# Turning v in 32x32 blocks on VectorE instead of TensorE, with adaLN rows loaded a step ahead and residual rows parked in DRAM

## Chip, cores, metric

The kernel runs on one core of a Trainium2 chip. The metric is the device time of one execution in microseconds (us). The core has TensorE (PE; its weight loads are shown apart as PEld), VectorE (DVE), ScalarE (ACT), GpSimd (POOL) and SyncE (SP). SP and ACT also issue DMAs, each on a queue of its own; an engine takes its instructions in order, so a DMA issue that waits holds up what stands behind it.

## What is computed

The reference is a backbone of two layers over 256 latent tokens that attend after 256 context tokens (512 together), model width 1024. Layer 0 mixes tokens by a Conformer convolution, layer 1 by a bidirectional mLSTM with 4 heads of 512. A squared-ReLU MLP of width 4096 follows in each layer, and shift, scale and gate of each half come from an adaLN map of a conditioning vector. All is float32. Cut to the part around the change:

```python
def adaln(cvec, w, b):
    return jnp.split(jax.nn.silu(cvec) @ w + b, 6, axis=-1)

def mlstm_features(u, ...):                     # MLSTM_INNER = 2048
    up = u @ w_up
    xm, z = up[..., :MLSTM_INNER], up[..., MLSTM_INNER:]
    xc = jax.nn.silu(dwconv(xm, w_conv) + b_conv)
    q, k, v = xc @ w_q, xc @ w_k, xm @ w_v
    gates = jnp.concatenate([q, k, v], axis=-1) @ w_gate + b_gate
    o = jax.nn.sigmoid(xm @ w_o + b_o)
    return xc, z, q, k, v, gates, o

# layer: x <- LN(ALPHA*x + gate * mixer(...)), then
h = layer_norm(ALPHA * h + g2 * sq_relu_mlp(modulate(h, sh2, sc2), ...), ...)
```

The scan then needs v with the tokens as rows (`scores @ v`, `k.T @ v` in chunks of 128 tokens).

## The kernel before

**Products.** Features lie on the 128 partitions and the 512 tokens in the free dimension. A float32 product is made of three fp32r matmuls: operands are split into a rounded part and a rest, and hi x hi, lo x hi and hi x lo are summed (`mm3` at L181, L184, L185; `mm3t`, with the operands exchanged, at L212 to L214; `mm_any` at L196, L197). Weights come from DRAM in tiles of 1 MB (`raw_load`, L144, on SP's queue, three buffers). ScalarE casts half a tile to `wh` (L150) and VectorE subtracts to get `wl` (L151); four pairs of them are in turn.

**Order.** A scheduler puts the instructions of every engine in one fixed order by dependencies and a model of costs; buffers come from pools, so a tile waits for the last reader of the buffer it reuses. Each DMA raises one of eight semaphores in turn, and an issue waits for the older DMA on its own one.

**The v stage** (about 719 to 926 us) computes v = xm @ w_v in 16 blocks of 128 output features, two at a time. `v_epi(m)` copies the finished block from PSUM to `vt` (ScalarE, L1215). Two blocks later `v_out` turns it: four transposes of 128x128 by TensorE into the PSUM tile `ln` (L1227), a ScalarE copy to `E` (L1229), and a store of 256 KB to `v_dr` in DRAM (L1230, ScalarE's queue). After every fourth block, so once a head, four gate matmuls per group (`gate_acc`, L1206) add v's part of the gates. Between the blocks of v stand the matmuls of w_q's transpose with the gate weights (`wgq_step`, L756), which end in a copy to `F` (L761) and transposes (L764). The q stage behind it begins with halves of `xc`, loaded, cast and split.

**adaLN rows.** `AdaV.step` multiplies rows of the adaLN map by the conditioning vector on VectorE: it loads a row tile `ar` of 256 KB (L418, SP's queue, one buffer, 80 times) and multiplies and adds it for each stream (L422 the first time, L426 afterwards). The first set runs during layer 0's MLP, the second (`ada_n2`) during v, q and k.

**Residual rows.** `R` (tile `res`, 128 x 2 x 1024, 1 MB) is filled by four ScalarE copies at 631 to 635 us (L1172). It is next read at 1354 us, when the mLSTM's down projection adds to it (L1648). The attention, with the o gates' weights (`gate_o`, `raw<-wo`), stands from about 1205 to 1475 us, then the second MLP.

Of the kernel before, what the change touches and what calls it, by code (L numbers as in the profile page):

```python
# [14 lines left out]
P = 128  # L15
# [7 lines left out]
H = 4  # L23
# [48 lines left out]
def hybrid_kernel(ctx: ExitStack, tc: tile.TileContext, xT, vecs_d, wdw_d, ada0_w, ada_w, wg_d, pw1a, pw1, pw2, w1_0, w2_0,  # L72
# [12 lines left out]
    def nm(s):  # L85
        uid[0] += 1
        return f"{s}_{uid[0]}"
# [3 lines left out]
    def tmp(tag, dt=F32):  # L91
        return tp.tile([P, T], dt, tag=tag, name=nm(tag), bufs={"E": 4, "S": 2, "L": 2, "F": 1}[tag])
# [8 lines left out]
    def psum(tag="mm"):  # L101
        return pp.tile([P, 512], F32, tag=tag, name=nm(tag), bufs={"mm": 3, "ln": 2, "fl": 1, "cv": 2}[tag])
# [297 lines left out]
    class AdaV:  # L400
# [3 lines left out]

        def __init__(self, l, units, streams, rows=()):
            self.l, self.units, self.streams, self.i, self.acc, self.todo = l, list(units) + list(rows), streams, 0, [], []
            self.ncol = len(units)

        def step(self):
            if self.todo:  # L410
                self.todo.pop(0)()
            n, kt = divmod(self.i, DT)
            if n == len(self.units):
                return
            if kt == 0:
                self.acc += [tmp("SL"[(len(self.acc) + i) // 2 % 2]) for i in range(len(self.streams))]
            w = adp.tile([P, 512], F32, tag="ar", name=nm("ar"))
            nc.sync.dma_start(w, ada_w[self.l, self.units[n], kt // 4, :, kt % 4 * 512:kt % 4 * 512 + 512])  # L418
            for i, s in enumerate(self.streams):
                a, c = self.acc[i - len(self.streams)], cs[:, kt, 14 + s:15 + s]  # L420
                if kt == 0:
                    o = nc.vector.tensor_scalar(a, w, c, None, op0=ALU.mult)  # L422
                    if i == 0:
                        tc.keep_in_program_order(o)
                else:
                    nc.vector.scalar_tensor_tensor(a, w, c, a, op0=ALU.mult, op1=ALU.add)  # L426
            self.i += 1
            if kt == DT - 1 and n < self.ncol and len(self.acc) == 4:
                accs, self.acc = self.acc, []
                u = self.units[n] + 1 - 4 // len(self.streams)  # L430
                self.todo += [lambda: self.sums(accs), lambda: None, lambda: self.end(u)]

        def flush(self):
            while self.todo:
# [725 lines left out]
    for _ in side:  # L1160
        pass

    R = xp.tile([P, 2, D], F32, name="res")
    for f in range(0, DT, 2):
        t, tr = tmp("S"), psum("cv")
        for i in range(2):
            nc.scalar.activation(t[:, i * C:(i + 1) * C], x[f + i][:, HI], AF.Identity, scale=al[:, 0, f + i:f + i + 1],
                                 bias=al[:, 1, f + i:f + i + 1])
            for tt in range(2):
                nc.tensor.transpose(tr[:, tt * C + i * P:tt * C + (i + 1) * P],  # L1170
                                    t[:, i * C + tt * P:i * C + (tt + 1) * P], ident)
        nc.scalar.copy(R[:, :, f * P:(f + 2) * P], tr.rearrange("p (t c) -> p t c", t=2))  # L1172

    xm = []

# [32 lines left out]
        seen.add(j)  # L1208

    wgv = gate_w(2, qc.tile([P, T], F32, name="wgv"))  # L1210
    vts = []

    def v_epi(m, ps):
        vt = B("vt").rearrange("p a b -> p (a b)")[:, :T]
# [6 lines left out]
    def v_out(m, vt):  # L1221
        if m % 4 == 3:
            for j in range(4):
                gate_acc(j, wgv[:, m - 3 + j, :], vts[m - 3 + j])
        tr = psum("ln")
        for b in range(4):
            nc.tensor.transpose(tr[:, b * P:(b + 1) * P], vt[:, b * P:(b + 1) * P], ident)  # L1227
        vk = tmp("E")
        nc.scalar.copy(vk, tr)  # L1229
        nc.scalar.dma_start(v_dr[m // 4][:, :, (m % 4) * P:(m % 4 + 1) * P], vk.rearrange("p (b c) -> p b c", b=4))  # L1230

    late = []

# [218 lines left out]
    def rows(dst, src):  # L1452
        nc.sync.dma_start(dst, src.broadcast_to([P, dst.shape[-1]]))
        return dst


    HF = [slice(0, 512), slice(512, 1024)]
    G1 = rows(qe.tile([P, D], F32, name="G1"), rows_d[0:1])
    for i in range(2):
        ada_n2.row(i, G1[:, HF[i]])  # L1460
    pw = {}
# [65 lines left out]
    def gate_o(h):  # L1527

        for d in range(2):
            bo = rows(BO().rearrange("p a b -> p (a b)"), bo_d[h:h + 1, d * DH:(d + 1) * DH])  # L1530
            pss = [psum() for _ in range(2)]
            for q in range(4):
                ws = preo if (h, d, q) == (0, 0, 0) else None
                if ws is None:
                    raw = raw_load(wo[h, d, q])
                for i in range(2):
                    w = ws[i] if ws else split_w(raw[:, i * 1024:(i + 1) * 1024])
                    for t in range(2):
                        for k in range(2):
                            kt = 4 * q + 2 * i + k  # L1540
                            sl = slice(k * 512, (k + 1) * 512)
                            mm3t(pss[t], xls[kt][0][:, BLK[t]], xls[kt][1][:, BLK[t]], w[0][:, sl], w[1][:, sl],
                                 kt == 0, kt == ET - 1)
                        if q == 3 and i == 1:
                            og[h, d, t] = o_ = OG()
                            nc.vector.tensor_tensor(o_, pss[t], bo, op=ALU.add)
                            nc.scalar.activation(o_, o_, AF.Sigmoid)
                    yield
# [368 lines left out]
    return v.reshape(-1, P).T  # L1917


def _layout(np, i):  # L1920
    g = {k: np.asarray(v) for k, v in i.items()}
    a = {}
    a["xT"] = np.concatenate([g["ctx"][0], g["x"][0]], axis=0).T
    vec = {
        "c_ctx": _cols(g["c_ctx"]), "c": _cols(g["c"][0]),
        "b_pw1": _cols(g["conv_b_pw1"][0]),
        "cln_g": _cols(g["conv_ln_g"][0]), "cln_b": _cols(g["conv_ln_b"][0]),
        "b_pw2": _cols(g["conv_b_pw2"][0]), "b_conv": _cols(g["ml_b_conv"][0]),
        "w_conv": g["ml_w_conv"][0].T.reshape(ET, P, QTAP).transpose(1, 0, 2).reshape(P, ET * QTAP),
        "gn_g": _cols(g["ml_gn_g"][0]), "skip": _cols(g["ml_skip"][0]),  # L1930
        "b_gate": np.tile(g["ml_b_gate"][0], (P, 4)),
    }
    for l in range(2):
        vec[f"ada_b{l}"] = _cols(g["ada_b"][l])
        for n in ("ln1_g", "ln1_b", "ln2_g", "ln2_b"):
            vec[f"{n}{l}"] = _cols(g[n][l])
    a["vecs_d"] = np.concatenate([vec[n] for n, _ in _VECS], axis=1)
    a["wdw_d"] = np.concatenate([g["conv_w_dw"][0], g["conv_b_dw"][0][None]], axis=0)
    aw = g["ada_w"].reshape(2, DT, P, 6 * D)
    a["ada_w"] = aw.reshape(2, 2, 4, P, 12, 512).transpose(0, 4, 1, 3, 2, 5).reshape(2, 12, 2, P, 2048)  # L1940
    a["ada0_w"] = aw[0, :, :, :2 * D].reshape(DT, P, 2, DT, P).transpose(3, 1, 0, 2, 4).reshape(DT, P, 2048)
    a["wg_d"] = g["ml_w_gate"][0].reshape(3, ET, P, 16).transpose(0, 2, 1, 3).reshape(3, P, 256)
    pw1 = g["conv_w_pw1"][0].reshape(D, 2, DT, P).transpose(0, 2, 1, 3)[:, :, ::-1, :].reshape(D, 2 * D)
    a["pw1a"] = pw1[:, :512].reshape(DT, P, 512)
    a["pw1"] = _blocks(pw1[:, 512:])
    a["pw2"] = _blocks(g["conv_w_pw2"][0])
    for l in range(2):
        a[f"w1_{l}"] = _blocks(g["mlp_w1"][l])
        a[f"w2_{l}"] = np.stack([_blocks(g["mlp_w2"][l][c * D:(c + 1) * D]) for c in range(4)])
    a["up_x"] = _blocks(g["ml_w_up"][0][:, :E])  # L1950
    a["up_z"] = _blocks(g["ml_w_up"][0][:, E:])
    a["wv"] = _blocks(g["ml_w_v"][0])
    a["wo"] = g["ml_w_o"][0].reshape(4, 4, P, 2, H, DH).transpose(4, 3, 0, 2, 1, 5).reshape(H, 2, 4, P, 2048)
    a["bo_d"] = g["ml_b_o"][0].reshape(2, H, DH).transpose(1, 0, 2).reshape(H, 2 * DH)
    a["wk"] = (g["ml_w_k"][0].T.reshape(2, 2, 4, P, 8, 2, P).transpose(0, 4, 3, 1, 5, 2, 6).reshape(2, 8, P, 2048))
    a["wq"] = _blocks(g["ml_w_q"][0])
    a["wqT"] = g["ml_w_q"][0].T.reshape(ET, P, E)
    a["wdown"] = g["ml_w_down"][0].reshape(H, 4, P, 2, 512).transpose(0, 3, 2, 1, 4).reshape(H, 2, P, 2048)
    a["w2_1"] = g["mlp_w2"][1].reshape(16, 2, P, D).transpose(0, 2, 1, 3).reshape(16, P, 2048)
    ab = g["ada_b"][1].reshape(6, D)  # L1960
    a["rows_d"] = np.stack([ab[2], ab[5], g["ln1_g"][1], g["ln1_b"][1], g["ln2_g"][1], g["ln2_b"][1]])
    return {k: np.ascontiguousarray(v) for k, v in a.items()}
# [23 lines left out]
```

## Time and profile before

| | before |
|---|---|
| median of 3 runs | 1670.03 us (1669.85 to 1670.98) |
| profiled execution | 1670.06 us |
| its span, first to last instruction | 1668.3 us |
| granted TensorE clock | 0.998 |
| TensorE busy | 1656.0 us, 8920 instructions |
| VectorE busy | 1030.2 us, 1857 instructions |
| ScalarE busy | 742.2 us, 1196 instructions |
| read from and written to DRAM | 284.37 MB and 15.77 MB |

A row of an engine's groups reads: line, engine, operation, output<-inputs, shape, count. A row of a waits view reads: engine and line that waited <- what it waited for: us in total, times, longest. Rows of a timeline or of the chain begin with the start and the length in us; a row with "x8" stands for eight instructions in a row, and its length for all of them. Matmuls overlap in TensorE, so the sum of their lengths is more than the time they take.

### The profile page before, as it was taken

The page shows a single profiled execution, that of the slowest core. Times are in us where ns is not written, and L with a number is a line of the kernel's source. Part 1 is how long each engine was busy: PE and PEld are TensorE (multiplying, and loading weights), DVE is VectorE, ACT ScalarE, POOL GpSimd, SP SyncE. Part 2 cuts the span into 40 slices and gives each one's busy share as a digit, 9 for nine tenths or more (in the row PEclk, how much of TensorE's full clock was granted, in tenths as well). Part 3 has the DMA queues.
Part 4 walks back from the last instruction along what each step waited for, and adds up shares of the span by engine and source line. Part 5 has one row for each costly group of instructions (what it writes and reads, how often), then busy time and mean ns, then how long its engine had stood idle before and what let it go on. Part 6 is the DMA issues. An engine that isn't in the chain of part 4 may idle for free.

```text
span 1668.3 us, 22876 instructions
## 1 busy us (share of the span) xinstructions
PE 1656.0 (99%) x8920; PEld 1364.9 (82%) x8920; DVE 1030.2 (62%) x1857; ACT 742.2 (44%) x1196; POOL 14.3 (1%) x64
## 2 busy tenths in 40 slices
PE   9999999999999999999999999999999999999998
PEld 6665898888888998877788899888878888878887
DVE  6555895666635765761143663564389876786677
ACT  4313573232324476652243532442368654655453
POOL 0000000000000000000000000000000000000001
PEclk9999999999999999999999999999999999999999
DMA  9565223444324064556775743455375556675552
GB/s 359 201 216 208 85 75 114 151 145 136 136 101 152 10 233 160 185 194 251 266 259 174 259 171 120 143 198 175 130 246 190 192 213 213 253 274 190 179 186 92
DMA packets 73901, 301.63 MB, mean 181 GB/s; under 512 B 7518, under 2 KB 23682, under 8 KB 43968
## 3 DMA queue, kind: packets, MB, share of 16 engines
q1 hardware_dynamic: 56080, 285.44, 48.3%
q10 hardware_dynamic: 17712, 14.72, 2.6%
q8 instruction: 70, 1.15, 0.3%
q14 instruction: 39, 0.32, 0.1%
HBM read 284.37 MB, written 15.77 MB: 180 GB/s over the span
## 4 chain that ended last, share of the span: by engine, by line
PE 96%; DVE 2%; DMA 1%; issue 0%; ACT 0%; SPq 0%; ACTq 0%; DVEq 0%
PE mm L181 17%; PE mm L184 17%; PE mm L185 17%; PE mm L196 7%; PE mm L212 4%; PE mm L214 4%; PE mm L213 4%; PE mm L197 4%; PE cv L212 2%; PE cv L214 2%; PE cv L213 2%; PE fl L343 1%; PE ln L181 1%; PE cv L839 1%; PE ln L184 1%; PE ln L185 1%
## 5 line engine op out<-in xcount | busy, mean ns | idle before, releaser
L151 DVE TENSOR_TENSOR wl<-raw,wh 128x1024 fp32r<-128x1024 f32 x344 | 418.9, 1222 | 276.2 <-ACT wh L150 263.5
L150 ACT CAST wh<-raw 128x1024 fp32r<-128x1024 f32 x344 | 358.7, 1051 | 502.3 <-PE mm L184 278.3
L184 PE MATMUL mm<-u,wh 128*128 128x512 f32 (+1 forms) x808 | 291.6, 361 | 0.2 <-DVE u L594 0.2
L181 PE MATMUL mm<-u,wh 128*128 128x512 f32 (+1 forms) x680 | 243.6, 359 | 0.0
L185 PE MATMUL mm<-u,wl 128*128 128x512 f32 (+1 forms) x680 | 241.3, 355 | 0.0
L184 PEld LDWEIGHTS mm<-u,wh 128*128 128x128 f32 x808 | 152.6, 189 | 22.2 <-DVE u L594 0.5
L181 PEld LDWEIGHTS mm<-u,wh 128*128 128x128 f32 x680 | 128.4, 189 | 25.2 <-issue 5.9
L185 PEld LDWEIGHTS mm<-u,wl 128*128 128x128 f32 x680 | 128.4, 189 | 18.6 <-issue 0.8
L212 PE MATMUL mm<-wh,xl 128*128 128x512 f32 x256 | 101.0, 395 | 0.1
L181 PE MATMUL mm<-xm,wh 128*128 128x512 f32 x256 | 101.0, 394 | 0.0
L213 PE MATMUL mm<-wh,xl 128*128 128x512 f32 x256 | 100.0, 391 | 0.0
L185 PE MATMUL mm<-xm,wl 128*128 128x512 f32 x256 | 99.7, 390 | 0.0
L214 PE MATMUL mm<-wl,xl 128*128 128x512 f32 x256 | 99.2, 391 | 0.0
L181 PE MATMUL mm<-hid,wh 128*128 128x512 f32 (+1 forms) x256 | 93.3, 364 | 0.0
L185 PE MATMUL mm<-hid,wl 128*128 128x512 f32 (+1 forms) x256 | 92.8, 363 | 0.0
L184 PE MATMUL mm<-hid,wh 128*128 128x512 f32 (+1 forms) x256 | 92.8, 363 | 0.0
L196 PE MATMUL mm<-x,wh 128*128 128x512 f32 x232 | 81.1, 398 | 0.0
L426 DVE SCALAR_TENSOR_TENSOR S<-ar,cs,S 128x512 f32<-128x512 f32 x56 | 40.8, 749 | 59.4 <-DMA ar<-ada_w 59.2
L184 PE MATMUL mm<-qq,wh 128*128 128x272 f32 x256 | 73.9, 289 | 0.0
L181 PE MATMUL mm<-qq,wh 128*128 128x272 f32 x256 | 73.5, 288 | 0.0
L185 PE MATMUL mm<-qq,wl 128*128 128x272 f32 x256 | 73.5, 288 | 0.0
L196 PE MATMUL mm<-u,wh 128*128 128x512 f32 x192 | 68.7, 399 | 0.0
(535 smaller groups left out, 3253.2 us busy)
## 6 DMA issues: line engine op xcount, KB each, us to landing
raw<-w SPq DMA_DIRECT2D x64, 1024.0 KB, 4.8
raw<-wo SPq DMA_DIRECT2D x32, 1024.0 KB, 4.8
raw<-ada_w SPq DMA_DIRECT2D x22, 1024.0 KB, 6.5
ar<-ada_w SPq DMA_DIRECT2D x80, 256.0 KB, 3.7
raw<-wv SPq DMA_DIRECT2D x16, 1024.0 KB, 6.8
raw<-wqT SPq DMA_DIRECT2D x16, 1024.0 KB, 6.2
raw<-wq SPq DMA_DIRECT2D x16, 1024.0 KB, 4.9
raw<-wk SPq DMA_DIRECT2D x16, 1024.0 KB, 5.1
```

What stands on the lines that cost most here:

```text
L150: c = nc.scalar.copy(hi, src)
L151: lastsub[0] = nc.vector.tensor_tensor(lo, src, hi.bitcast(F32), op=ALU.subtract).ins
L181: a = nc.tensor.matmul(ps, wh, xh, start=start, stop=False)
L184: nc.tensor.matmul(ps, wh, xl, start=False, stop=False)
L185: lastmm[0] = nc.tensor.matmul(ps, wl, xh, start=False, stop=stop).ins
L196: todo = [lambda s_, e_: nc.tensor.matmul(ps, wh, r[0], start=s_, stop=e_), lambda s_, e_: nc.tensor.matmul(ps[:, :n], wl, r[0][:, :n], st ...
L197: lambda s_, e_: nc.tensor.matmul(ps[:, :n], wl, r[0][:, :n], start=s_, stop=e_)]
L212: nc.tensor.matmul(ps, xh, wh, start=start, stop=False)
L213: nc.tensor.matmul(ps, xl, wh, start=False, stop=False)
L214: nc.tensor.matmul(ps, xh, wl, start=False, stop=stop)
L343: a = mark_unit[0] = nc.tensor.matmul(ps[32 * j:32 * j + 32], cs[:, kt, 14 - 2 * v:46 - 2 * v], blocks[kt], start=first and kt < 4, stop=l ...
L426: nc.vector.scalar_tensor_tensor(a, w, c, a, op0=ALU.mult, op1=ALU.add)
```

## The change

Three things change.

1. v is no longer turned by TensorE. VectorE turns each `vt` block of 128x512 in blocks of 32x32 within the four groups of 32 partitions, directly into a tile `res` of 1 MB that holds one head. After the head's fourth block four DMAs, each from 32 partitions and of 256 KB, store it to `v_dr`. So that a 32x32 turn gives whole rows, the host permutes the columns of w_v within each head, and the rows of w_gate that belong to v. 64 transposes and 16 ScalarE copies are gone.
2. `AdaV.step` loads the next row tile before it uses the present one; `ar` has two buffers.
3. `R` is stored to DRAM (`r_dr`) after it is filled, so that the one `res` buffer can serve v, and loaded again on SP's queue in the first `gate_o`, behind its first weight tile.

```diff
 # class AdaV, step and load
-            n, kt = divmod(self.i, DT)
+            n, kt = divmod(self.i - len(self.loads), DT)
...
-            w = adp.tile([P, 512], F32, tag="ar", name=nm("ar"))
-            nc.sync.dma_start(w, ada_w[self.l, self.units[n], kt // 4, :, kt % 4 * 512:kt % 4 * 512 + 512])
+            w = self.loads.pop(0) if self.loads else self.load()
+            if self.i < DT * len(self.units):
+                self.loads.append(self.load())
...
-            self.i += 1
...
+        def load(self):
+            n, kt = divmod(self.i, DT)
+            w = adp.tile([P, 512], F32, tag="ar", name=nm("ar"), bufs=2)
+            nc.sync.dma_start(w, ada_w[self.l, self.units[n], kt // 4, :, kt % 4 * 512:kt % 4 * 512 + 512])
+            self.i += 1
+            return w

 # residual rows
-    R = xp.tile([P, 2, D], F32, name="res")
+    def rows_tile():
+        return xp.tile([P, 2, D], F32, tag="res", name=nm("res"), bufs=1)
+
+    r_dr = dp.tile([P, 2, D], F32, name="r_dr")
+    R = rows_tile()
...
         nc.scalar.copy(R[:, :, f * P:(f + 2) * P], tr.rearrange("p (t c) -> p t c", t=2))
+    nc.scalar.dma_start(r_dr, R)

 # v_out
-        tr = psum("ln")
-        for b in range(4):
-            nc.tensor.transpose(tr[:, b * P:(b + 1) * P], vt[:, b * P:(b + 1) * P], ident)
-        vk = tmp("E")
-        nc.scalar.copy(vk, tr)
-        nc.scalar.dma_start(v_dr[m // 4][:, :, (m % 4) * P:(m % 4 + 1) * P], vk.rearrange("p (b c) -> p b c", b=4))
+        if m % 4 == 0:
+            vturn.append(rows_tile().rearrange("p a b -> p (a b)").rearrange("p (t m j) -> p t m j", m=4, j=32))
+        vk = vturn[-1]
+        nc.vector.transpose(vk[:, :, m % 4, :], vt)
+        if m % 4 == 3:
+            for q in range(4):
+                r = slice(32 * q, 32 * q + 32)
+                nc.scalar.dma_start(v_dr[m // 4][:, :, q * P:(q + 1) * P].rearrange("(q i) b x -> i b q x", i=32),
+                                    vk[r].rearrange("i (b q) m j -> i b q (m j)", b=4))

 # attention
+    R = rows_tile()
...
             pss = [psum() for _ in range(2)]
+            if (h, d) == (0, 1):
+                with tc.issue_after(loaded[0]):
+                    nc.sync.dma_start(R, r_dr)

 # host
+def _turned(np):
+    return np.arange(DH).reshape(4, 4, 32).transpose(1, 0, 2).reshape(DH)
...
+    wg = g["ml_w_gate"][0].reshape(3, H, DH, 16)
+    wg = np.stack([wg[0], wg[1], wg[2][:, turned]])
...
-    a["wv"] = _blocks(g["ml_w_v"][0])
+    a["wv"] = _blocks(g["ml_w_v"][0].reshape(E, H, DH)[..., turned].reshape(E, E))
```

Line numbers shift with the added code: L1206 becomes L1218, L1215 becomes L1227, L756 becomes L763, L418 becomes L436. The block transposes stand at L1240, the stores of v at L1244, the reload of R at L1550.

On TensorE, at the end of head 0, the order before reads so (`fl` and `wgq` belong to w_q's gate product, `cv` sums the gates):

```order
3839 L184 MATMUL mm_6996<-x_6678,wh_7070 128x512
3840 L185 MATMUL mm_6996<-xm_6677,wl_7071 128x512
3841 L1227 MATMUL ln_7100<-ident,vt_6936 128x128 x4
3842 L1206 MATMUL cv_6693<-vt_6789,wgv 32x512
3843 L1206 MATMUL cv_6693<-vt_6832,wgv 32x512
3844 L1206 MATMUL cv_6693<-vt_6936,wgv 32x512
3845 L1206 MATMUL cv_6693<-vt_6994,wgv 32x512
3846 L1227 MATMUL ln_7112<-ident,vt_6994 128x128 x4
3847 L756 MATMUL fl_6791<-raw_7120,wgq_578 32x512 x4
```

The same place on TensorE now:

```order
3837 L184 MATMUL mm_6985<-x_6680,wh_7059 128x512
3838 L185 MATMUL mm_6985<-xm_6679,wl_7060 128x512
3839 L1218 MATMUL cv_6695<-vt_6791,wgv 32x512
3840 L1218 MATMUL cv_6695<-vt_6834,wgv 32x512
3841 L1218 MATMUL cv_6695<-vt_6938,wgv 32x512
3842 L1218 MATMUL cv_6695<-vt_6983,wgv 32x512
3843 L763 MATMUL fl_6793<-raw_7099,wgq_578 32x512 x4
```

Both groups of four transposes are gone, and the matmuls around them stand as they did. On VectorE, in the same stretch and up to the second head (`res_6940` is head 0, `res_7245` head 1, in one buffer), there now stands:

```order
838 L151 TENSOR_TENSOR wl_6990<-raw_6987,wh_6989 128x1024
839 L1240 STREAM_TRANSPOSE res_6940<-vt_6938 128x16x32
840 L151 TENSOR_TENSOR wl_7030<-raw_6987,wh_7029 128x1024
841 L1240 STREAM_TRANSPOSE res_6940<-vt_6983 128x16x32
842 L151 TENSOR_TENSOR wl_7060<-raw_7057,wh_7059 128x1024
843 L151 TENSOR_TENSOR wl_7112<-raw_7057,wh_7111 128x1024
844 L1240 STREAM_TRANSPOSE res_7245<-vt_7087 128x16x32
845 L151 TENSOR_TENSOR wl_7146<-raw_7143,wh_7145 128x1024
```

Before, only the `wl` steps stood there. The transpose in row 844 writes the buffer that the stores of head 0 read, and a `wl` stands behind it. On SP, in the attention's first steps, the queue now reads:

```order
271 L144 DMA raw_10765<-wo 128x2048
272 L1468 DMA G_10634<-rows_d 128x1024
273 L1468 DMA bo_10695<-bo_d 128x512
274 L144 DMA raw_10830<-wo 128x2048
275 L144 DMA raw_10885<-wo 128x2048
276 L1550 DMA res_10636<-r_dr 128x2048
277 L144 DMA raw_10951<-wo 128x2048
278 L144 DMA raw_11007<-wo 128x2048
```

The reload of R (row 276) stands behind the third of these `wo` loads; before, the loads of `wo` followed each other there without it.

More of the change, by code (lines that the diff above doesn't have):

```diff
@@ L406, in __init__ @@
             self.l, self.units, self.streams, self.i, self.acc, self.todo = l, list(units) + list(rows), streams, 0, [], []
-            self.ncol = len(units)
+            self.ncol, self.loads = len(units), []
         def step(self):
@@ L1210, in hybrid_kernel @@
     wgv = gate_w(2, qc.tile([P, T], F32, name="wgv"))
-    vts = []
+    vts, vturn = [], []
     def v_epi(m, ps):
@@ L1917, in _cols @@
     return v.reshape(-1, P).T
+def _turned(np):
+    return np.arange(DH).reshape(4, 4, 32).transpose(1, 0, 2).reshape(DH)
 def _layout(np, i):
     g = {k: np.asarray(v) for k, v in i.items()}
-    a = {}
+    a, turned = {}, _turned(np)
     a["xT"] = np.concatenate([g["ctx"][0], g["x"][0]], axis=0).T
@@ L1941, in _layout @@
     a["ada0_w"] = aw[0, :, :, :2 * D].reshape(DT, P, 2, DT, P).transpose(3, 1, 0, 2, 4).reshape(DT, P, 2048)
-    a["wg_d"] = g["ml_w_gate"][0].reshape(3, ET, P, 16).transpose(0, 2, 1, 3).reshape(3, P, 256)
+    wg = g["ml_w_gate"][0].reshape(3, H, DH, 16)
+    wg = np.stack([wg[0], wg[1], wg[2][:, turned]])
+    a["wg_d"] = wg.reshape(3, ET, P, 16).transpose(0, 2, 1, 3).reshape(3, P, 256)
     pw1 = g["conv_w_pw1"][0].reshape(D, 2, DT, P).transpose(0, 2, 1, 3)[:, :, ::-1, :].reshape(D, 2 * D)
```

## The prediction

> **What bounds the kernel now.** I read the page first: how busy each engine is, and of what the chain that ended last consists.
>
> ```profile
> PE 1656.0 (99%) x8920; PEld 1364.9 (82%) x8920; DVE 1030.2 (62%) x1857; ACT 742.2 (44%) x1196; POOL 14.3 (1%) x64
> PE 96%; DVE 2%; DMA 1%; issue 0%; ACT 0%; SPq 0%; ACTq 0%; DVEq 0%
> ```
>
> TensorE is busy for 99% of the span and makes 96% of the chain. The waits of TensorE come next, longest first.
>
> ```profile
> PE cv L175 <- DVE ones L129: 1.1, 1, 1.1
> PE fl L343 <- DMA raw<-ada_w: 0.9, 2, 0.7
> PE ln L963 <- DVE u L869: 0.4, 1, 0.4
> PE fl L764 <- ACT F L761: 0.4, 1, 0.4
> ```
>
> No wait adds up to more than 1.1 us. So a wait that the change removes can bring next to nothing; what can bring time is TensorE work that goes, and what can cost time is a new wait of TensorE. Last I read the busy time by stage, in windows of the v stage (719 to 926 us), of its end, and of the attention (columns: PE, PEld, DVE, ACT, POOL, clock, DMA share, GB/s).
>
> ```profile
> 760.00:780.00 20.00, 20.00 (x107) 13.96 (x106) 4.81 (x4) 6.14 (x8) 0.00 (x0) 1.00 0.66 235
> 780.00:800.00 20.00, 20.00 (x104) 14.57 (x103) 2.36 (x2) 4.15 (x6) 0.00 (x0) 1.00 0.68 265
> ...
> 920.00:940.00 20.00, 20.00 (x113) 15.79 (x112) 12.92 (x24) 12.00 (x24) 0.00 (x0) 1.00 0.83 272
> 1240.00:1260.00 20.00, 20.00 (x90) 16.26 (x88) 18.83 (x45) 17.04 (x33) 0.00 (x0) 1.00 0.47 148
> 1260.00:1280.00 20.00, 20.00 (x94) 16.67 (x93) 18.99 (x40) 13.52 (x24) 0.00 (x0) 1.00 0.64 230
> ```
>
> In the v stage VectorE works 2.4 to 4.8 of 20 us, ScalarE 4 to 6: both have room. In the attention VectorE works 19 of 20 us: there is no cover there.
>
> **The change, part by part.**
>
> *The 64 transposes leave TensorE.* The group's row, and the pieces of the chain that hold them:
>
> ```profile
> L1227 PE MATMUL ln<-ident,vt x64: 270/272/328, 760.9 to 923.5; 128*128 128x128 f32 x64
> ...
> 761.03 0.87 PE ln L1227 x8
> 787.88 0.44 PE ln L1227 x4
> 789.31 0.59 PE ln L1227 x4
> 867.58 0.87 PE ln L1227 x8
> 914.05 0.87 PE ln L1227 x8
> ```
>
> One record lasts 272 ns, but the records overlap: on the chain eight in a row take 0.87 us, 0.109 us each. Where they stand around the gate matmuls (L1206) they come as 0.44 + 0.59 = 1.03 us for eight. There are eight groups of eight (16 blocks of v, two at a time), four of either kind: 4 x 0.87 + 4 x 1.03 = 7.6 us. The bounds: 64 x 0.109 = 7.0 us, if the 0.59 holds 0.15 us of a drain that stays with L1206, and 9.2 us, the page's busy time of the group (below), if the records' own sum counts. I take 7.6, because the chain counts what delays the next piece.
>
> [...]
>
> *The 16 copies of L1229 leave ScalarE; 16 block transposes of 128x512 come to VectorE.* The trace of before has no such transpose. The nearest rows, fp32 operations of 128x512 on VectorE:
>
> ```profile
> L422 DVE TENSOR_SCALAR S<-ar,cs x8: 476/482/486, 280.2 to 1116.4; 128x512 f32<-128x512 f32 x8
> L426 DVE SCALAR_TENSOR_TENSOR S<-ar,cs,S x56: 743/751/754, 284.1 to 1152.1; 128x512 f32<-128x512 f32 x56
> L1227 PE MATMUL ln<-ident,vt 128*128 128x128 f32 x64 | 9.2, 276 | 0.0
> L1229 ACT COPY E<-ln x16: 580/592/606, 762.1 to 923.8; 128x512 f32<-128x512 f32 x16
> ```
>
> 0.48 to 0.75 us each: 8 to 12 us in all, over 190 us in which VectorE is mostly idle. I take 0.5, and zero for the end. What such a step could delay is the next wl (L151), behind it in order. The wl of this stage are early:
>
> ```profile
> 776.95 2.36 DVE L151 TENSOR_TENSOR wl<-raw,wh 128x1024 fp32r<-128x1024 f32 x2 [10.57 <-ACT wh L150]
> ...
> 782.73 0.39 PE L185 MATMUL mm<-xm,wl 128*128 128x512 f32 x1
> ```
>
> The first of these two is done 1.23 us after 776.95, at 778.18, and TensorE first reads it at 782.73: 4.55 us in hand, the least of the stage. A step of 0.75 us disappears in it; without that cover it would cost 16 x 0.75 = 12 us. ScalarE gains 16 x 0.59 = 9.5 us, which nobody waits for, save once: at 833 TensorE waits 0.4 us for F (L761), and the chain leads there from two L1229 copies and their stores ahead of a wh cast. That 0.4 us may go; I leave it in the range.
>
> *Four stores a head instead of sixteen small steps.* Bytes are the same, 16 x 256 KB on ScalarE's queue, but each now leaves from 32 partitions.
>
> ```profile
> L1230 ACTq DMA_DIRECT2D v_dr<-E x16: 520/521/1424, 762.7 to 924.5; - x16
> ...
> DMA to landing us min/median/max: 2.4/4.1/14.0
> ...
> 769.53 0.59 ACT L1215 COPY vt<-mm 128x512 f32<-128x512 f32 x1 [4.40 <-PE mm L185]
> 789.33 0.59 ACT L1215 COPY vt<-mm 128x512 f32<-128x512 f32 x1 [1.58 <-PE cv L1206]
> ```
>
> The new wait is VectorE's: the next head's first transpose overwrites the one `res` buffer, so all four stores must have landed. Head 0 is complete with the copy of 769.53, and the next block comes at 789.33: 19.8 us later. Transpose, four issues of 0.52 us and a median landing need 0.6 + 0.6 + 2.1 + 4.1 = 7.4 us; with the longest landing of before, 17.3 us. Behind the waiting transpose stands wl, with its 4.55 us. So 24.35 us are there for 7 to 17: cost 0, above only if landings from 32 partitions double.
>
> [...] No row of before shows such a store.
>
> On ScalarE four issues stand in a row, and behind them a wh cast, or at the end of the stage the casts of xc:
>
> ```profile
> 921.14 0.58 ACT L1215 COPY vt<-mm 128x512 f32<-128x512 f32 x1
> ...
> 921.27 1.23 DVE L151 TENSOR_TENSOR wl<-raw,wh 128x1024 fp32r<-128x1024 f32 x1 [0.89 <-ACT wh L150]
> ...
> 924.33 0.41 ACT L150 CAST xc<-raw 128x256 fp32r<-128x256 f32 x1
> ...
> 925.46 2.44 DVE L151 TENSOR_TENSOR xc<-raw,xc 128x256 fp32r<-128x256 f32 x7 [0.27 <-ACT xc L150]
> ...
> 930.37 0.39 PE L196 MATMUL mm<-xc,wh 128*128 128x512 f32 x1
> ```
>
> Now the last v block, copied by 921.72, is turned behind a wl that ends at 922.50 (done by 923.2 at 0.75 us), and four issues of 0.52 us follow before the first xc cast: 925.3 instead of 924.33. The last of the eight xc halves was split at 927.90, and TensorE began with the first at 930.37, so 2.5 us or more are in hand for a delay of 1. Cost 0; from above 1 us, should the last issue wait for an older transfer too.
>
> *The rows of AdaV a step ahead.* VectorE waits for them now:
>
> ```profile
> DVE S L426 <- DMA ar<-ada_w: 59.2, 31, 3.8
> ```
>
> 31 waits go or shrink, but TensorE waits for no result of them. Gain 0, cost 0: the load goes out a step earlier on SP's queue, its buffer is the one freed a step before.
>
> *R out and in again.* The store (1 MB, ScalarE's queue, at 635 us) lies in a stage where nothing waits for ScalarE's transfers. The reload stands on SP's queue among the wo loads.
>
> ```profile
> raw<-wo SPq DMA_DIRECT2D x32, 1024.0 KB, 4.8
> 1208.51 18.08 SPq L144 DMA_DIRECT2D raw<-wo x6
> 1217.57 1.04 ACT L150 CAST wh<-raw 128x1024 fp32r<-128x1024 f32 x1
> ...
> 1223.79 0.39 PE L212 MATMUL mm<-wh,xl 128*128 128x512 f32 x1
> ...
> L1648 DVE TENSOR_TENSOR res<-res,E x4: 683/688/692, 1354.2 to 1368.0; 128x512 f32<-128x512 f32 x4
> ```
>
> R itself is needed at 1354, some 135 us later. The wo loads behind it come up to 4.8 us later. The cast of 1217.57 ends at 1218.6, TensorE uses it at 1223.79: 5.2 us. So 0, from above 4.8 us, should the delay carry into the tight part.
>
> *The order in the attention.* There the scheduler sets some matmuls and VectorE steps otherwise. TensorE has hardly any slack in it:
>
> ```profile
> 1290.14 1.21 DVE L151 TENSOR_TENSOR wl<-raw,wh 128x1024 fp32r<-128x1024 f32 x1
> ...
> 1291.40 0.50 PE L214 MATMUL mm<-wl,xl 128*128 128x512 f32 x1
> ```
>
> This wl ends at 1291.35 and TensorE takes it 0.05 us later. A step that now stands before or behind such a wl shifts TensorE by its own length, 0.5 to 1.2 us by the rows of VectorE here. One such step gained or two lost is what I allow: minus 1 to plus 2 us. The value is 0, since the same steps are all still there.
>
> Sum: the profiled execution took 1670.06 us (span 1668.3, 1.76 around it), 0.03 over the median of the three runs. 1670.06 - 7.6 = **1662.5 us**.
>
> **The rivals.**
>
> *Given back in the attention.* VectorE, 19 of 20 us busy from 1240 to 1280, cannot catch up, and the late wo weights become waits of TensorE. Price up to 4.8 us, one landing: 1662.5 + 4.8 = 1667.3. For it: the slack of 0.05 us at 1291. Against: 5.2 us in hand at 1217, and a DMA share of 0.47 from 1240 to 1260, room to catch up.
>
> *Nothing freed.* TensorE's weights come no faster than now, and the 7.6 us turn into waits for wl: 1670. For it: DMA share 0.66 to 0.68. Against: weights lie ready 4.55 us and more, and their loads wait for buffers that TensorE frees, so they move up with it.
>
> *Slower: one buffer for turned v.* If a head's stores land later than 24.35 us after its last copy, VectorE stands at the next head's first transpose, wl behind it, and TensorE at wl. Three heads follow another. At 28.5 us (the 14 us landing twice over, and a little) it is 4.15 x 3 = 12.5 us: 1675. The end exceeds 1673.4 from 28 us on. Against: a median landing of 4.1 us.
>
> *The record's length as price.* If each transpose held TensorE for its 272 ns, 64 x 0.272 = 17.4 us would go: 1652.7. [...] Against: eight take 0.87 us on the chain; the trace speaks clearly.
>
> **How the numbers follow.** A measurement of this kernel can tell 0.2% from no change, 3.3 us. Chances: forecast 0.78, with its own spread from 1659.5 (9.2 us for the transposes, 0.4 for F, 1 in the attention) to 1665.5 (7.0 and the costs of 2 and of 0.5 us); given back 0.11; nothing freed 0.04; slower 0.04; the record's length 0.03. Given back ends on either side of 1666.7, so I split it, 0.03 faster and 0.08 same. Faster: 0.78 + 0.03 + 0.03 = 0.84; same: 0.08 + 0.04 = 0.12; slower 0.04. The range takes in the forecast's spread and given back: 1659.5 to 1667.5.
>
> **What would show it right or wrong.** Right: no transpose of v on TensorE, its busy time and the span both lower by 7 to 8 us, the first xc matmul of the q stage at about 923 instead of 930.37, and the stages behind it as long as before; the block transposes at 0.5 to 0.75 us; no wait of TensorE for wl in the v stage. Wrong: a wait of VectorE on the stores at the first block of a head; a landing of stores over 20 us; a span from 1205 to 1300 that grew by over 2 us; TensorE's waits summing to more than the few us of now.

## The result, and the profile after

Over ten executions each, the changed kernel took 1666.09 us at the median (1664.22 to 1668.59) and the kernel before 1670.26 (1669.73 to 1671.7): ratio 0.9975, 95% interval 0.9967 to 0.9984. That is 4.2 us less where 7.6 was forecast; the sign and the range held, the size was a little over half. In four later runs the same kernel came out at 1664.92, 1664.76, 1665.6 and 1665.23 (ratios 0.9965 to 0.9973). All 34 executions have their median at 1665.2.

The profiled execution after took 1664.27 us, its span 1662.6, against 1670.06 and 1668.3: 5.8 us less. The page's first lines (busy time by engine, and what the chain that ended last consists of):

```profile
PE 1649.9 (99%) x8856; PEld 1357.6 (82%) x8856; DVE 1040.0 (63%) x1873; ACT 733.7 (44%) x1180; POOL 14.4 (1%) x64
PE 95%; DVE 3%; DMA 1%; ACT 0%; issue 0%; SPq 0%; DVEq 0%; ACTq 0%
```

TensorE has 64 matmuls fewer and 6.1 us less work, VectorE 9.8 us more, ScalarE 8.5 less. TensorE still makes nearly all of the chain. Its waits, longest first, next:

```profile
PE cv L175 <- DVE ones L129: 1.1, 1, 1.1
PE fl L343 <- DMA raw<-ada_w: 0.9, 2, 0.7
PE mm L212 <- DVE og L1565: 0.7, 1, 0.7
PE ln L970 <- DVE u L876: 0.4, 1, 0.4
```

The wait for F at the end of w_q's gate product (0.4 us) is gone; a wait for og, in the attention, is new. Where the time went shows best at one matmul that both kernels have, the first of the attention's wo products. Before, then after, from the timeline (start, length):

```profile
1205.81 0.79 PE L212 MATMUL mm<-wh,xl 128*128 128x512 f32 x1
```

```profile
1198.13 0.79 PE L212 MATMUL mm<-wh,xl 128*128 128x512 f32 x1
```

There the changed kernel is 7.68 us ahead. Compared matmul by matmul (the starts of the same matmul in two traces, one taken from the other), 0.24 of it stood before the v stage, and 0.56 came where TensorE had waited for F (833 us). That wait is gone too in the two versions below that turn v as before (0.60 and 0.59 us at the same matmul), so its going can't be put down to the turned v. The transposes are left with 6.9 us, 0.108 each. At the matmul that stood at 1300 us before, the lead is down to 6.6 us, behind the attention it is 6.1, and at the end of the span 5.7. So the v stage brought nearly what was forecast, and in this execution the attention took 1.6 us back, 1.1 of it by 1300 us. The block transposes, their stores, and VectorE's waits in the changed kernel:

```profile
L1240 DVE STREAM_TRANSPOSE res<-vt x16: 700/706/712, 735.5 to 915.3; 128x512 f32<-128x512 f32 x16
L1244 ACTq DMA_DIRECT2D v_dr<-res x16: 577/686/2070, 769.8 to 918.0; - x16
...
DMA to landing us min/median/max: 3.6/6.3/12.3
```

```profile
DVE res L1240 <- DMA v_dr<-res: 3.5, 1, 3.5
```

A transpose takes 0.706 us, inside the bounds of 0.48 to 0.75 and near the upper. A store of 32 partitions lands after 6.3 us at the median instead of 4.1, 1.5 times as late; the longest is no longer than before. VectorE waited once for the stores of a head, 3.5 us at 890, and TensorE has no wait between 700 and 1000 us.

### The profile page after: what moved, and what is told of

Its sections match the earlier page's. It is cut to its first block, busy times and chain, and to the rows that moved or that the text cites. A ratio compares the mean times of both kernels' runs of the same rounds, so it can differ in the third digit from the quotient of the medians.

```text
span 1662.6 us, 22739 instructions
## 1 busy us (share of the span) xinstructions
PE 1649.9 (99%) x8856; PEld 1357.6 (82%) x8856; DVE 1040.0 (63%) x1873; ACT 733.7 (44%) x1180; POOL 14.4 (1%) x64
## 4 chain that ended last, share of the span: by engine, by line
PE 95%; DVE 3%; DMA 1%; ACT 0%; issue 0%; SPq 0%; DVEq 0%; ACTq 0%
PE mm L181 18%; PE mm L184 17%; PE mm L185 17%; PE mm L196 7%; PE mm L197 4%; PE mm L214 4%; PE mm L212 4%; PE mm L213 3%; PE cv L212 2%; PE cv L214 1%; PE cv L213 1%; PE fl L343 1%; PE ln L181 1%; PE cv L846 1%; PE ln L184 1%; PE fl L763 1%
## 5 line engine op out<-in xcount | busy, mean ns | idle before, releaser
L1078 DVE SCALAR_TENSOR_TENSOR x<-mm,ada,x 128x256 f32<-128x256 f32 x64 | 28.5, 479 | 64.0 <-PE mm L185 63.8
```

The source lines that it names most:

```text
L1078: nc.vector.scalar_tensor_tensor(res[m][:, sl_], p_, g[:, m:m + 1], res[m][:, sl_], op0=ALU.mult, op1=ALU.add)
```

## The experiments

**The adaLN rows, without and alone.** The first version is the changed kernel with the class `AdaV` of before; the second is the kernel before with the new one.

```diff
-            w = self.loads.pop(0) if self.loads else self.load()
-            if self.i < DT * len(self.units):
-                self.loads.append(self.load())
+            w = adp.tile([P, 512], F32, tag="ar", name=nm("ar"))
+            nc.sync.dma_start(w, ada_w[...])
```

> The changed kernel with the adaLN rows loaded when they are used, as before (one ar buffer); TensorE's order is the changed kernel's. Theory: TensorE never waits for these rows, so the time is that of the changed kernel, 1664 to 1668 us with the same spread, within 0.5 us of its median 1666.1. Rival: loading ahead collides with the weight loads and causes the spread of the changed kernel; then this version lies at 1664.3 with little spread. Second rival: loading ahead gains; then this version is slower by 1 us or more.

Measured: 1664.51 us (1664.04 to 1667.87, six executions), 0.9969 of the kernel before (0.9958 to 0.9981). That overlaps the changed kernel: loading ahead neither gains nor costs anything that can be told. One of the six is some 3 us longer than the others, at a mean clock of 0.997, so loading ahead doesn't make such executions (more on them below).

> The kernel before with only the adaLN rows loaded a step ahead. Theory: 0, so 1670.3 us within 0.5, VectorE's waits for ar fall from 78 us to some 35. Rival (those waits reach TensorE somewhere): 1 us or more faster.

Measured: 1669.88 us, ratio 0.9999 (0.999 to 1.0008). VectorE's waits for `ar`, in the kernel before and in this one:

```profile
DVE S L426 <- DMA ar<-ada_w: 59.2, 31, 3.8
DVE L L426 <- DMA ar<-ada_w: 15.1, 9, 3.4
```

```profile
DVE S L427 <- DMA ar<-ada_w: 34.8, 18, 4.7
DVE L L427 <- DMA ar<-ada_w: 12.2, 6, 4.6
```

Some 27 us of waits went (47 us are left, where some 35 were expected), and the time stayed.

**R stored and reloaded, alone.** The kernel before with these lines:

```diff
+    nc.scalar.dma_start(r_dr, R)
...
+            if (h, d) == (0, 1):
+                with tc.issue_after(loaded[0]):
+                    nc.sync.dma_start(R, r_dr)
```

> The kernel before with only R stored and reloaded; v is still turned by TensorE. Theory (the attention gives back about 2 us because of the reload and of the order that it brings): 1671.5 to 1672.5 us, with the added time between 1200 and 1310 us. Rival (the reload is hidden and the loss belongs to the order that comes with the turned v): 1670.3 within 0.5.

Measured: 1671.7 us (1670.91 to 1672.64) beside 1670.35 in the same job, ratio 1.0008 (0.9999 to 1.0017). The median is 1.35 us up, at the edge of what can be told, as the theory had it. The added time is in the attention: compared matmul by matmul with the profile of before, TensorE loses 1.25 us between 1205 and 1300 us. It waits there as follows, and VectorE is busy for the whole window (last row; columns as in the windows of the prediction).

```profile
PE ln L1402 <- DVE E L1388: 0.8, 1, 0.8
PE mm L212 <- DVE og L1555: 0.4, 1, 0.4
...
1240.00:1260.00 20.00, 19.60 (x87) 15.90 (x86) 20.00 (x49) 17.25 (x33) 0.00 (x0) 1.00 0.55 185
```

**The transposes alone.**

```diff
-        tr = psum("ln")
-        for b in range(4):
-            nc.tensor.transpose(tr[:, b * P:(b + 1) * P], vt[:, b * P:(b + 1) * P], ident)
         vk = tmp("E")
-        nc.scalar.copy(vk, tr)
+        nc.scalar.copy(vk, vt)
```

> The kernel before without the 64 transposes of v: ScalarE copies vt itself to E and all else stays, so v reaches DRAM unturned and the scan's numbers are other ones. Theory (each transpose costs TensorE 0.11 to 0.13 us): 7.0 to 8.0 us less, 1662.3 to 1663.3. Rival (transposes were partly free): 1666. Rival (the record's length is the price): 1653.

Measured: 1663.95 us (1663.35 to 1665.24), ratio 0.9961 (0.9947 to 0.9975): 6.4 us less than 1670.35, a little short of the theory's 7.0 to 8.0. In its profiled execution, the longest of the five at 1665.24 us, the first wo matmul starts at 1199.06 instead of 1205.81:

```profile
1199.06 0.79 PE L212 MATMUL mm<-wh,xl 128*128 128x512 f32 x1
```

These 6.75 us are a net figure. Compared matmul by matmul, the first seven eights of transposes save 0.83 to 1.11 us each, 6.3 us in all, 0.113 per transpose. Another 0.56 is the wait for F, gone here as well. At the last eight a new wait takes the saving back:

```profile
PE cv L1206 <- ACT vt L1215: 0.9, 1, 0.9
```

Then it loses 1.7 us in the attention, though its matmuls and VectorE steps stand there in the order of before and nothing is reloaded. Waits from the attention's start on:

```profile
PE ln L1394 <- DVE E L1380: 1.0, 1, 1.0
PE mm L212 <- DVE og L1543: 0.4, 1, 0.4
PE mm L212 <- ACT wh L150: 0.3, 1, 0.3
```

So part of what the attention can take back belongs neither to the reload nor to the new order.

Sum of the parts at the medians: minus 6.4 for the transposes, minus 0.5 (not to be told from 0) for the rows, plus 1.35 for R: minus 5.5, or 1664.8 us. The changed kernel's 34 executions have 1665.2.

**The longer executions.** The ten executions of the result lay in two groups, five at 1664.2 to 1665.2 us with a mean clock of 0.999 and five at 1667.0 to 1668.6 with 0.996 to 0.998. I ran the kernel again, and two versions beside it.

> The changed kernel again. Its ten executions lay in two groups, 1664.2 to 1665.2 us and 1667.0 to 1668.6, the second with a mean granted clock of 0.996 to 0.997 in place of 0.999. Theory: in the longer ones TensorE waits for wl in the v stage, because VectorE stands at a load of adaLN rows or at the stores of a head (in the profile of a short one the slack was down to 0.66 us at 841 us), and the clock then drops for a few us; the two groups come again, and a profile of a long one shows the gap between 830 and 900 us. Rival: the longer ones lose their 3 us in the attention (1200 to 1310 us), at the reload of R.

Measured: 1664.92 us (1663.85 to 1666.17), no long execution, so the profile could not decide.

The second version takes the adaLN rows out of the v stage:

```diff
-        if vstep > ET:
-            ada_n2.step()
...
-            if i % 2:
-                ada_n2.step()
+            ada_n2.step()
```

> The changed kernel without steps of the second adaLN's rows in the v stage; they run in the q stage instead, at every step and not at every second. Theory (VectorE's line of row loads and turned blocks holds up wl in the v stage): only the short group is left, median 1664.0 us, all within 1.5 us. Rival (attention or reload): two groups as in the changed kernel, median 1665 to 1667.

Measured: 1673.5 us (1670.43 to 1675.13), ratio 1.0016 (1.0007 to 1.0025). Both theories missed: the q stage has no room for these steps. VectorE waits for a row, the split of q (`qq`) stands behind it, TensorE waits 4 us, and from 967 to 978 us the granted clock (third number from the end) is about half:

```profile
PE mm L184 <- DVE qq L151: 4.0, 1, 4.0
...
960.00:967.00 7.00, 4.92 (x34) 4.39 (x33) 3.68 (x5) 2.85 (x6) 0.00 (x0) 1.00 0.87 251
967.00:978.00 11.00, 7.25 (x30) 6.92 (x31) 7.32 (x15) 2.17 (x5) 0.00 (x0) 0.53 0.62 233
```

It says nothing on the v stage. But it shows a drop of the clock at a wait of TensorE: 1.00 up to 967 us, 0.53 over the 11 us in which the wait of 4 us ended.

The third moves the reload of R to the second head's o gates:

```diff
-            if (h, d) == (0, 1):
+            if (h, d) == (1, 0):
```

> The changed kernel with the reload of R in the second head's o gates instead of the first's, some 60 us later and still ahead of its use. Theory (the longer executions come from the v stage, the reload costs 1 us): two groups remain, each 1 us lower: 1663.5 and 1666.5. Rival (the reload among the first wo loads makes the longer executions): one group, 1663.5 to 1664.5.

Measured: 1664.43 us (1663.89 to 1667.92), ratio 0.9967. Its profiled execution is a long one, 1667.92 us. My theory of the v stage fell: there is no gap of TensorE there. The gap is at the attention's entry, before the reload is even issued. ScalarE's cast of the second wo load, the wait at the decay matmuls, and the clock:

```profile
1208.24 2.00 ACT L150 CAST wh<-raw 128x1024 fp32r<-128x1024 f32 x2 [3.61 <-DMA raw<-wo]
...
1216.32 0.39 PE L212 MATMUL mm<-wh,xl 128*128 128x512 f32 x1
1218.61 0.49 PE L1412 MATMUL ln<-E,tri 128*128 128x128 f32 x2 [1.91 <-DVE E L1398]
...
1221.49 0.63 PE L213 MATMUL mm<-wh,xl 128*128 128x512 f32 x1
...
1219.00:1223.00 4.00, 4.00 (x14) 3.25 (x14) 2.05 (x7) 0.00 (x0) 0.00 (x0) 0.57 0.75 289
```

The load was issued at 1201.05 and its cast could begin only at 1208.24; in the changed kernel's first profile it was issued at 1200.82 and cast at 1206.04. ScalarE stood for it 3.61 us instead of 1.64. VectorE's chain of small steps to E (L1398) ends 2 us later than in a short execution of the same version (1663.15 us, at the end of this section), TensorE waits 1.91 us, and then 3.4 us run at half clock: a matmul takes 0.63 us instead of 0.39. Compared matmul by matmul with that short execution, this one is 3.6 us behind at 1222 us, 1.9 of waiting and 1.7 of half speed, and 0.9 more follows by 1249.

Three more runs went to this.

> The changed kernel a third time, for the share and the place of its longer executions. Theory, from the profile of a long execution of the version with the later reload: at the entry of the attention the second wo load lands up to 2 us late, the chain of VectorE steps behind it ends late, TensorE waits 1.9 us at the decay matmuls (L1412), and the granted clock is halved for 3.4 us; a long execution here shows the same, near 1219 us. Rival (another place, such as the head ends of the v stage): a clock drop elsewhere. Short ones 1664 to 1666 us, long ones 1667 to 1669.

> The changed kernel a fourth time, to find one of its longer executions in a profile (5 of 20 so far). Theory: it shows a wait of TensorE of about 2 us at the decay matmuls (L1412) at the attention's entry, behind a wo load that landed some 2 us late, and a half clock for 3 to 4 us after it. Rival: a clock drop elsewhere. A short one shows neither; 1664 to 1666 us.

> The same once more: a longer execution shows the late wo load, the wait at L1412 and the half clock by the theory; a clock drop elsewhere by the rival. Short ones 1664 to 1666 us.

Measured: 1664.76, 1665.6 and 1665.23 us; one long execution among 19 (1668.45, clock 0.997), and no profile fell on it. But the profiles show the same wait in smaller sizes. ScalarE's cast of the second wo load with its idle time, and TensorE's wait at L1412 where there is one, for the changed kernel's executions of 1664.27, 1664.91, 1665.31 and 1666.22 us, in this order:

```profile
1206.04 2.00 ACT L150 CAST wh<-raw 128x1024 fp32r<-128x1024 f32 x2 [1.64 <-DMA raw<-wo]
```

```profile
1206.97 2.00 ACT L150 CAST wh<-raw 128x1024 fp32r<-128x1024 f32 x2 [1.97 <-DMA raw<-wo]
...
PE ln L1412 <- DVE E L1398: 0.4, 1, 0.4
```

```profile
1207.14 2.00 ACT L150 CAST wh<-raw 128x1024 fp32r<-128x1024 f32 x2 [2.33 <-DMA raw<-wo]
...
PE ln L1412 <- DVE E L1398: 0.7, 1, 0.7
```

```profile
1207.50 2.01 ACT L150 CAST wh<-raw 128x1024 fp32r<-128x1024 f32 x2 [2.95 <-DMA raw<-wo]
...
PE ln L1412 <- DVE E L1398: 1.4, 1, 1.4
```

The longer ScalarE stands for the load, the longer TensorE waits: 0, 0.4, 0.7 and 1.4 us, and 1.9 us with a drop of the clock in the long execution above. The fifth profile of the changed kernel (1664.76 us) fits, with 1.25 us for the load and no wait. The time follows in part only. The four differ from the first by 0, 0.6, 1.0 and 2.0 us; of this 0, 0.6, 0.4 and 0.1 stood before the v stage, and 0, 0.3, 0.7 and 1.3 came between the first wo matmul and 1222 us.

Nor is this wait bound to the turned v. ScalarE's and TensorE's times are 1.95 and 0.2 us in the kernel before, 1.56 and 0 with the rows alone, 2.36 and 0.8 with R alone, 2.68 and 1.0 without the transposes, 1.48 and 0 in the changed kernel without rows ahead. Only the version with the rows after v is out of line, with 1.59 and 0.4.

To see whether a late load makes the clock drop in any version, I put a copy of 1 MB right ahead of it in the kernel before:

```diff
+            if (h, d) == (0, 0):
+                with tc.issue_after(last_row[0]):
+                    nc.sync.dma_start(dp.tile([P, 2048], F32, name="junk"), wo[0, 0, 0])
```

> The kernel before with one copy of 1 MB from DRAM to DRAM on SP's queue right ahead of the second wo load of the attention; nothing else is added, and the scheduler sets the attention's order anew for it. Theory (a wo load that lands late there makes TensorE wait, and over some 2 us the clock drops too, in any version): 2 to 6 us longer, 1672 to 1676, with a mean clock of 0.997 or below and the gap at 1225 us. Rival (the drop belongs to the turned v and its order): 1670.3 to 1671.5 with a clock of 0.999.

Measured: 1676.55 us (1676.37 to 1677.91), ratio 1.004 (1.0026 to 1.0053): 6.5 us longer, more than the theory's upper end, at a clock of 0.997 to 0.999. It is inconclusive on the clock: the scheduler moved the decay chain behind other work, and TensorE waits in other places, with no drop there in the profiled execution (a granted clock of 1.00 in each window of 20 us from 1195 to 1295 us) although one wait is 2.7 us long:

```profile
PE mm L212 <- ACT wh L150: 2.7, 1, 2.7
PE mm L212 <- DVE og L1551: 1.4, 1, 1.4
```

What it does show: 1 MB more at the attention's entry, together with the order that the scheduler then set, costs 6.5 us. How much is the copy's and how much the order's is not told apart.

**The later reload again.**

> The version with the reload of R in the second head's o gates again. Theory (the reload costs little where it stands, and the longer executions don't hang on it): 1664 to 1665 us, a longer one now and then. Rival (one long profile was chance and the later reload saves 1 us): median 1663.7 or below.

Measured: 1663.87 us (1663.15 to 1667.91), ratio 0.9965 (0.9952 to 0.9977), beside 1665.6 and 1665.23 of the changed kernel in the same job; the first time 1664.43 beside 1664.92. The intervals overlap, so a gain of some 1 us over the changed kernel is likely and not settled. Two things differ, the place of the reload and the order: with the later reload every engine has the attention's order of before (all 2206 matmuls between 1150 and 1600 us stand in the same order), while the changed kernel and the version with R alone have another.

In the profiles, VectorE's wait for the rows `L<-ng_dr`, which stand on SP's queue behind the wo loads, first with the reload among these, then with it later:

```profile
DVE S L1502 <- DMA L<-ng_dr: 2.4, 1, 2.4
```

```profile
DVE S L1502 <- DMA L<-ng_dr: 1.1, 1, 1.1
```

In the first, VectorE has hardly a pause from that wait at 1230 to og at 1248 (the chain of waits runs through VectorE all that way), and TensorE waits 0.7 us for og. In the second no wait of TensorE is left between 1190 and 1320. The wait of 0.7 us for og stands in all five profiles of the changed kernel, whether the second wo load was late or not. But the rows alone do not explain it. VectorE waits as long for them in the long execution of the version with the later reload (first), and in the version without the transposes (second), where nothing is reloaded. Both have the order of before and a late second wo load:

```profile
DVE S L1502 <- DMA L<-ng_dr: 2.3, 1, 2.3
```

```profile
DVE S L1483 <- DMA L<-ng_dr: 2.3, 1, 2.3
```

TensorE waits 0.4 us for og in each of these. So whether the early reload costs its 1 us by itself, by these rows or by the order that comes with it stays open. No other version that was run had a lower median.

## Why the prediction was right, and where its size failed

*The transposes.* Right: 0.108 us each in the changed kernel and 0.113 over seven eights alone (the forecast's lower bound was 0.109), not the record's 0.272. I took 7.6 us, 1.03 for the eights around the gate matmuls; 6.9 came, so the bound of 7.0 was the better value. That the lead at the first wo matmul was 7.68 us is in part luck: 0.24 of it stood before the v stage and 0.56 is the wait for F, which I had left in the range and which also went where v was turned as before.

*The signs.* The first xc matmul came at 923.76 us, as forecast (about 923), and no wait for wl stands in the v stage. TensorE's busy time fell by 6.1 us and the span by 5.7, not by 7 to 8. One sign of being wrong came: VectorE waited for the stores at the first block of a head.

*VectorE and ScalarE in the v stage.* Right: 16 x 0.706 = 11.3 us at no cost, four issues in a row at no cost. The margin shrank more than I said, though. I had stores landing at up to 17.3 us after a head's last copy and no wait; VectorE did wait 3.5 us at head 3, because head 2's last block was turned at 874.8 only, behind a step that waited for an adaLN row, and a store then landed up to 12.3 us after its issue, 20.6 us after the head's last copy. The stores took 6.3 against 4.1 us to land at the median, 1.5 times; they leave from 32 partitions and four in a row, and the two are not told apart. The rival of the one buffer was on the right track and short of its price.

*The rows a step ahead.* Right: 0.

*R, and the attention: the step that failed.* I set the reload at 0 with an upper bound of 4.8, and the order at 0 with minus 1 to plus 2. I judged both by slack in one execution (5.2 us at 1217) and looked for wo weights that the reload makes late. The runs show something else. First, the reload and the order that comes with it make TensorE wait 0.7 us for og in every profile of the changed kernel. By the medians they cost some 1 us (1.35 with R alone, 0.5 to 1.7 against the later reload); how the cost divides between the two is not shown. Second, the entry of the attention: the second wo load varies by 2 us from one execution to the next (7.19 us from issue to cast in the long execution above, 5.22 in the first profile of the changed kernel), and a serial chain of ScalarE and VectorE steps carries that to TensorE, which waits 0 to 1.9 us. The kernel before has that wait too (0.2 us in its profile), so it is no cost of the change alone; but what I measured the change by is the median, and half of the ten executions of the result were long.

*The rival "given back in the attention"* (0.11) came nearest to the result: 1667.3 forecast, 1666.1 measured. Its mechanism held in part: VectorE's steps come late, and at the entry a late wo load is behind them, but not one that the reload had delayed. The result lies above the forecast's own spread (up to 1665.5), in the part of the range that this rival added. There was chance in that: of the next 24 executions of the same kernel one was long, where five of these ten were.

What stays open: why a long execution turned up in 9 of 50 with turned v (the changed kernel, the version without rows ahead, the later reload), while none of 60 executions of the kernel before had a mean clock below 0.998. One was caught in a profile, and its cause is seen there; that the others have the same is likely by their time and clock, and not shown.

## What to carry to other kernels

Where one engine is busy 99% of the span, count the work taken from it at the pace of the pipeline (start to start), not at the records' length: 0.108 us against 0.272 here. Then look at what comes after: a tight stage passed a late load on here. At the attention's entry VectorE was busy for 7.99 of 9 us in the long execution (1210 to 1219 us), the second wo load came 2 us late, and TensorE waited 1.91. In the attention the time at which a transfer's own data are needed does not tell what adding it costs: R was needed some 135 us later, and its reload with the order that came with it cost some 1 us. Judge slack in more than one execution; one profile shows one draw of the loads' landing times.

## What was not expected of the hardware

In the long execution of the version with the later reload a wait of TensorE of 1.91 us was followed by 3.4 us at half the granted clock (0.57 over 1219 to 1223 us, matmuls at 0.63 instead of 0.39 us), so that it cost nearly double: 1.9 us of waiting and 1.7 of half speed. Not every wait is followed by such a stretch: in the version with the added copy a wait of 1.4 us and one of 2.7 us had none. The windows around the wait of 1.91 us, then those around the waits of 1.38 and 2.71 us (columns as in the windows of the prediction):

```profile
1216.00:1219.41 3.41, 1.50 (x8) 0.78 (x7) 3.38 (x13) 1.39 (x2) 0.00 (x0) 1.00 0.46 159
1219.41:1222.83 3.42, 3.42 (x12) 2.94 (x13) 1.64 (x3) 0.00 (x0) 0.00 (x0) 0.50 0.72 273
1223.00:1230.00 7.00, 6.93 (x32) 5.31 (x31) 5.74 (x10) 3.89 (x4) 0.00 (x0) 1.00 0.57 232
```

```profile
1255.00:1260.00 5.00, 3.69 (x15) 2.77 (x16) 5.00 (x13) 4.65 (x9) 0.00 (x0) 1.00 0.23 63
1260.00:1265.00 5.00, 3.95 (x21) 3.03 (x20) 2.35 (x8) 4.93 (x9) 0.00 (x0) 1.00 0.82 252
1265.00:1270.00 5.00, 3.15 (x12) 2.29 (x13) 5.00 (x14) 4.18 (x12) 0.00 (x0) 1.00 0.18 29
1270.00:1275.00 5.00, 4.37 (x19) 3.25 (x18) 5.00 (x12) 3.10 (x5) 0.00 (x0) 1.00 0.61 234
```

The wait of 1.91 us ended at 1218.61, and the window from 1219.41 to 1222.83 has a clock of 0.50. The wait of 2.71 us ended at 1266.66, with a clock of 1.00 in all four windows. So in these runs the length of a wait alone does not tell whether the clock drops; what decides it is not shown.
